# Four edits to a two-layer encoder kernel: a sum order, a prologue order, the diagonal of the row scales, and the value projection of two heads

## The chip, the cores and the metric

One core of a Trainium2 chip runs the whole program in one launch. Its engines are PE (TensorE, the matrix engine), DVE (VectorE), ACT (ScalarE), POOL (GpSimd) and SP (SyncE, which here only starts transfers). Each engine works through its own instruction stream in order and waits at semaphores for the others. The metric is device time in microseconds (us) of the one core, the median of several executions.

## What is computed

The reference takes a sequence of 512 tokens of 1024 features and applies two layers. In the first the mixer is multi-head latent attention (MLA, 16 heads in 8 pairs, chunk-causal), in the second an mLSTM matrix memory (4 heads of 128 query and key features and 256 value features). Behind each mixer stands a feed-forward network (FFN).

```python
for i in range(DEPTH):                       # DEPTH = 2
    hn = rms_norm(x, norm_mix[i])
    y = mla_mixer(hn, ...) if i == 0 else mlstm_mixer(hn, ...)
    x = x + y
    x = x + sqrelu_mlp(rms_norm(x, norm_ffn[i]), ffn_w1[i], ffn_w2[i])

def mlstm_mixer(h, w_in, w_if, b_if, head_norm, w_o):
    q, k, v, o_pre = jnp.split(h @ w_in, [hq, 2 * hq, 2 * hq + hv], axis=-1)
    gates = (h @ w_if + b_if).astype(jnp.float32)
    ...
def sqrelu_mlp(h, w1, w2):
    return jnp.square(jax.nn.relu(h @ w1)) @ w2
```

## The kernel before

**Splits.** Every large product runs in fp32r. Each factor is split into a high part (a cast, usually on ACT) and a low part (a subtraction, on DVE or POOL), and one product becomes three matmuls on PE (`mm3`): high by high, high by low, low by high. A weight is loaded by a transfer into `wr` or `tw`, cast into `wh` and subtracted into `wl`. So each weight passes a transfer, ACT, and DVE or POOL before PE uses it.

**Stages.** The program runs MLA from 0 to about 245 us, the first FFN to about 578, the mLSTM to about 790, and the second FFN to the end. Tokens lie in four blocks of 128, features in eight blocks of 128. In the FFNs and in the MLA the engines keep the order in which the code was written; in most of the mLSTM a scheduler orders the instructions of each engine.

**The MLA prologue.** The string `START` names the work on the first pairs of heads one unit at a time, and each engine takes its share in that order. A unit is a letter, a pair and a token block. W splits a pair's weights (cast on ACT, low part on DVE for the queries and on POOL for the keys and values). P projects (15 matmuls of 256 columns; a small p is the same into another bank). A squares, B makes the statistics (on POOL the small operations `sm` and `scr`), C scales into the tile `f` (two heads on DVE, the rotary half of the keys on POOL). X turns `f` (four transposes on PE, tile `tp`), x splits the result. S, s, M, E and N are scores and softmax of the first head. e, R, r, g and h make and turn the low-rank inputs of a token block. Behind the string comes a loop with its own fixed order, which begins with T0, the turn of the first head's probabilities.

**The FFN.** The second matrix of the FFN is multiplied in chunks by a scheme of seven products on quarter blocks (a Strassen scheme). Its right factors are sums of quarters of the weight; the kernel forms them in transfers that add to what lies in memory (`s_sum`, `l_sum`, all issued from POOL). For the last chunk the factors t1 to t4 lie in two tiles named `z`, which are first filled with the quarter b12 and then take one or more added quarters. t4 takes three, b11, b22 and b21, one behind the other. The left factors are four subtractions on POOL (`z<-z`, x4). The products of a chunk are added to the residual rows `x` by DVE (`y_add`). The last two products of the last chunk, numbers 5 and 6, use t3 and t4, split into the tiles `zw`. Between their halves PE turns the finished rows `x` for the next stage (`mm<-cst,x`), which DVE and ACT scale into `xg`.

**The mLSTM.** The values of a head are projected with 256 columns (264 for head 0, whose weight `w_v0` holds the gates as well), from two weight tiles per head. `rows_sb` spreads the norms of the tokens over all partitions: it makes a diagonal from them and multiplies it by ones.

Of the kernel before, what the change touches and what calls it, by code (L numbers as in the profile page):

```python
# [61 lines left out]
def trunk(ctx: ExitStack, tc, a, yT, dbg=None):  # L62
# [33 lines left out]
    def tmp(dt=F32):  # L96
        return ph[0].tile([P, 512], dt, tag="t", bufs=tb[0], name=nm("t"))
# [87 lines left out]
            c = slice(off + k * stride, off + k * stride + m)  # L185
            mm3(out, hi[:, c], lo[:, c], rhs[k][0], rhs[k][1], k == 0, k == n - 1)

    def rows(r):

        dg = tmp()  # L190
        for t in range(NB):
            nc.vector.tensor_scalar_mul(dg[:, t * P:(t + 1) * P], ident, r[:, t:t + 1])
        ps = ps_tp()
        pe.matmul(ps, lhsT=ones, rhs=dg, start=True, stop=True)
        return ps

# [59 lines left out]
    def mla(mp):  # L256
# [340 lines left out]
                 "T": p_bank, "t": p_split, "V": pv, "o": o_split}  # L597
        ORDER = ("S0 s0 P0 S1 S2 T0 X0 s1 T1 s2 D1 A0 T2 P1 M0 E0 t0 B0 t1 t2 E2 E3 A1 E1 V0 x0 X1 V1 V2 W0 V3 N0 C0 B1 x1 o0")

        START = ("W00 Z00 Z01 g00 e00 g01 Z02 R00 h00 r00 e01 Z04 g02 P00 R01 h01 A00 Z03 e02 r01 B00 W10 R02 g03 h02 C00 r02 P01 X00 A01 e03 R03 P02 B01 h03 r03 A02 C01 B02 P03 P10 x00 X01 C02 x01 A03 B03 X02 p11 x02 S01 C03 A10 P12 S00 X03 B10 W20 s01 A11 C10 X10 x03 s00 S02 A12 B11 s02 p13 M00 B12 C11 X11 x10 E00 E02 A13 B13 E01 E03 C12 N00 C13 x11")  # L600
        PRO = {"Z": lambda t: z_mm((((0, 0), (0, 1)), ((1, 0), (1, 1)), ((2, 1), (3, 1)), ((3, 0),), ((2, 0),))[t], range(KD - ZL, KD)), "e": z_out, "R": z_turn, "Q": lambda t: z_turn(t, True), "r": z_split,
               "h": z_rope, "g": z_stat}

# [119 lines left out]
    def ffn(fp, layer, last):  # L723
# [181 lines left out]
        for s_ in range(2, len(units) - 2):  # L905
            u = units[s_]
            if u[0] == "F":
                ps = ps_mm()
                f_mm(ps, u[1])
                ws.pop(u)  # L910
            else:
                post = s_mm(u[1], u[2])
            ahead(s_)
            s_now[0] = s_
            while later and later[0][0] <= s_:
                later.pop(0)[1]()
            if u[0] == "F":
                f_post(ps, u[1])
                if u[1] == 4 * NC - 2:
                    l_load()  # L920
                if s_ < 5:
                    norm.square(s_ - 1, 0)
                    norm.square(s_ - 1, 1)
                    if s_ == 4:
                        idve.reciprocal(r2[:, 0], norm.stat())
                        idve.tensor_scalar_mul(r2[:, 1], r2[:, 0], -1.0)
            else:
                post()
                c, k = u[1], u[2]
                if c == NC - 1:  # L930
                    pass
                elif c == NC - 2:
                    if k == 2:
                        s_load(c + 1, ("b11",))
                    elif k == 3:
                        l_sum(("t1", "b11"), ("t2", "b11"), ("t3", "b22"), ("t4", "b11"))
                    elif k == 5:
                        s_load(c + 1, ("b21", "b22"))
                        l_sum(("t2", "b22"), ("t4", "b22"))
                    elif k == 6:  # L940
# [45 lines left out]
    def mlstm(lp):  # L986
# [16 lines left out]
        def gates(gps):  # L1003
# [45 lines left out]
            nc.vector.tensor_scalar_mul(cs, r, DK ** -0.5)  # L1049
            G["cs"] = cs  # L1050

        for h in range(MH):
            nv = DV + (2 * MH if h == 0 else 0)
            src = a["w_v0"] if h == 0 else a["w_v"][h - 1]
            ws = [load_w(src[c], 4 * nv, nc.gpsimd if h == 0 else nc.vector) for c in range(2)]
            vh, vl = vt[2 * (h % 2)], vt[2 * (h % 2) + 1]
            nc.gpsimd.memset(vh.bitcast(F32)[:, :, DV:], 1.0)
            nc.gpsimd.memset(vl.bitcast(F32)[:, :, DV:], 0.0)
            gps = []
            for t in range(NB):  # L1060
                tk = slice(t * P, (t + 1) * P)
                ps = ps_mm()
                for k in range(KD):
                    hi, lo = ws[k // 4]
                    c = slice((k % 4) * nv, (k % 4 + 1) * nv)
                    mm3(ps[:, :nv], xg[k][0][:, tk], xg[k][1][:, tk], hi[:, c], lo[:, c], k == 0, k == KD - 1,
                        ipe if h == 0 else pe)
                if h == 0 and t == 0:
                    iact.on = True
                    for do in norm.tail:  # L1070
                        do()
                    for i in range(2):
                        norm.square(2 + i, 0)
                    iact.on = False
                    roots(1)
                nc.scalar.activation(vh[:, t, 0:DV], ps[:, 0:DV], AF.Copy, scale=r[:, t:t + 1])
                nc.vector.scalar_tensor_tensor(vl[:, t, 0:DV], ps[:, 0:DV], r[:, t:t + 1],
                                               vh.bitcast(F32)[:, t, 0:DV], op0=mult, op1=sub)
                if h == 0:
                    gs = small(2 * MH)  # L1080
                    nc.vector.tensor_copy(gs, ps[:, DV:nv])
                    gps.append(gs)
            if h == 0:
                gates(gps)
                R = rows_sb(r)
# [122 lines left out]
def _layout(i):  # L1208
    def f(n):
        return np.asarray(i[n], dtype=np.float32)  # L1210

    def tiles(w):

        k, m = w.shape
        return w.reshape(k // P, P, m // P, P).transpose(2, 1, 0, 3).reshape(m // P, P, k)

    def cols(w):

        k, m = w.shape
# [60 lines left out]
```

## Time and profile before

| | |
|---|---|
| Median of 3 runs | 1130.61 us (1129.76 to 1131.3) |
| The profiled execution, its own time | 1130.33 us |
| Its span, first to last instruction | 1128.6 us |
| PE busy | 1107.3 us, 98% |
| DVE, ACT, POOL busy | 68%, 50%, 32% |
| Mean granted TensorE clock | 0.995 of full speed |

The span leaves 1.7 us around it. A row of a timeline gives the start, the length, the engine, the line, the operation, the tile written and the tiles read, their size, and how many like instructions stand together; in square brackets is the idle time of the engine ahead of it and what ended that. Line 80 is a helper that records instructions in order, so most rows carry it and the tiles tell the place. Matmuls overlap, so the spacing of their starts says more than their length.

### The profile page before, as it was taken

To read this page: it belongs to the slowest core of one execution; us is meant where nothing else is said; L and a number is where in the kernel's file an instruction comes from. 1 tells how busy PE (TensorE), PEld (TensorE's weight loads), DVE (VectorE), ACT (ScalarE), POOL (GpSimd) and SP (SyncE) were. 2 spreads that over 40 slices of the span, in tenths; PEclk is the share of its full clock that TensorE was granted. 3 is DMA by queue.
4 is the path that set the end of the run, shared out by engine and by line. 5 is a ranking of instruction groups with operands and counts; after the bars stand their busy time and mean duration, and the time that the engine had idled before them with its cause. 6 is when DMAs were issued, how large, how long until landed. Compare 5 with 4: busy or idle time off the path is not lost.

```text
span 1128.6 us, 15807 instructions
## 1 busy us (share of the span) xinstructions
PE 1107.3 (98%) x5790; PEld 949.1 (84%) x5790; DVE 763.3 (68%) x1308; ACT 568.0 (50%) x1004; POOL 363.4 (32%) x481
## 2 busy tenths in 40 slices
PE   9899999999999999999999999999999999999998
PEld 8889988888888888888798898888888888888876
DVE  5689997455676776776776465554476776767567
ACT  4478876437444544444465344332654545444442
POOL 3567785203332323324330011000323224224250
PEclk9899999999999999999999999999999999999999
DMA  9201021455666676575923223222675575666575
GB/s 323 72 25 48 20 76 38 131 170 127 170 151 149 165 154 146 151 174 149 203 71 102 86 58 92 81 90 81 197 170 130 159 180 131 164 168 139 160 153 127
DMA packets 44669, 146.23 MB, mean 130 GB/s; under 512 B 4912, under 2 KB 8368, under 8 KB 44592
## 3 DMA queue, kind: packets, MB, share of 16 engines
q1 hardware_dynamic: 34512, 108.52, 30.6%
q0 software_dynamic: 10080, 36.70, 19.2%
q8 instruction: 46, 0.75, 0.3%
q14 instruction: 31, 0.25, 0.1%
HBM read 143.11 MB, written 2.10 MB: 129 GB/s over the span
## 4 chain that ended last, share of the span: by engine, by line
PE 90%; DMA 3%; DVE 3%; POOL 2%; ACT 1%; issue 1%; SPq 0%; ACTq 0%; DVEq 0%; POOLq 0%
PE mm L80 40%; PE tp L80 34%; PE mm L178 4%; PE mm L177 4%; PE mm L176 4%; PE po L80 3%; DMA z<-in_w 1%; DMA wr<-in_w_z 1%; DVE x L80 1%; PE tp L178 1%; PE tp L177 1%; PE tp L176 1%; DMA t<-in_x 1%; POOL z L80 0%; POOL x L80 0%
## 5 line engine op out<-in xcount | busy, mean ns | idle before, releaser
L80 PE MATMUL mm<-xg,wh 128*128 128x512 f32 (+1 forms) x1088 | 318.9, 377 | 0.0
L80 POOL TENSOR_TENSOR z<-z 128x256 f32<-128x256 f32 x128 | 145.1, 1153 | 348.3 <-ACT z L80 345.8
L80 PEld LDWEIGHTS mm<-xg,wh 128*128 128x128 f32 x1088 | 200.1, 188 | 37.5
L80 PE MATMUL mm<-xg,wl 128*128 128x512 f32 (+1 forms) x544 | 204.9, 377 | 0.0
L80 DVE TENSOR_TENSOR wl<-tw,wh 128x1024 fp32r<-128x1024 f32 x104 | 134.5, 1293 | 87.9 <-ACT wh L80 87.9
L80 PE MATMUL tp<-wh,hh 128*128 128x512 f32 x424 | 165.3, 390 | 4.7 <-DVE x L80 4.7
L80 PE MATMUL tp<-wh,hl 128*128 128x512 f32 x424 | 165.0, 389 | 0.0
L80 PE MATMUL tp<-wl,hh 128*128 128x512 f32 x424 | 165.0, 389 | 0.0
L80 DVE TENSOR_TENSOR wl<-wr,wh 128x1024 fp32r<-128x1024 f32 (+1 forms) x72 | 94.0, 1306 | 102.1 <-ACT wh L80 102.1
L80 DVE SCALAR_TENSOR_TENSOR x<-tp,r,x 128x512 f32<-128x512 f32 (+1 forms) x223 | 155.2, 735 | 2.6 <-PE tp L80 2.5
L80 ACT ACTIVATE t<-mm 128x512 f32<-128x512 f32 (+3 forms) x97 | 54.3, 559 | 185.5 <-PE mm L80 179.5
L80 ACT CAST wh<-tw 128x1024 fp32r<-128x1024 f32 x104 | 108.9, 1047 | 40.5 <-DMA tw<-in_w 23.7
L80 PEld LDWEIGHTS mm<-xg,wl 128*128 128x128 f32 x544 | 102.4, 188 | 18.9 <-DVE wl L80 0.4
L80 PEld LDWEIGHTS tp<-wh,hh 128*128 128x128 f32 x424 | 79.6, 188 | 22.6 <-issue 3.5
L80 ACT CAST wh<-wr 128x1024 fp32r<-128x1024 f32 (+1 forms) x74 | 79.0, 1067 | 29.9 <-PE tp L80 25.5
L80 PEld LDWEIGHTS tp<-wh,hl 128*128 128x128 f32 x424 | 79.6, 188 | 16.6
L80 PEld LDWEIGHTS tp<-wl,hh 128*128 128x128 f32 x424 | 79.6, 188 | 16.5
L80 POOL DMA_DIRECT2D tw<-in_w x56 | 49.1, 876 | 124.4 <-DVE wl L80 112.4
L166 DVE TENSOR_TENSOR wl<-wr,wh 128x1024 fp32r<-128x1024 f32 (+1 forms) x39 | 45.7, 1173 | 56.3 <-ACT wh L162 55.5
L162 ACT CAST wh<-wr 128x1024 fp32r<-128x1024 f32 (+2 forms) x42 | 41.9, 1001 | 63.1 <-PE mm L177 31.6
L80 ACT ACTIVATE hh<-z 128x1024 fp32r<-128x1024 f32 x32 | 34.0, 1064 | 71.5 <-POOL z L80 71.5
L80 PE MATMUL mm<-wh,big 128*128 128x256 f32 (+1 forms) x256 | 58.2, 306 | 0.0
(286 smaller groups left out, 2096.5 us busy)
## 6 DMA issues: line engine op xcount, KB each, us to landing
wr<-in_w SPq DMA_DIRECT2D x64, 512.0 KB, 3.7
tw<-in_w SPq DMA_DIRECT2D x62, 512.0 KB, 4.2
tw<-in_w POOLq DMA_DIRECT2D x56, 512.0 KB, 5.7
z<-in_w POOLq DMA_DIRECT2D x14, 512.0 KB, 7.7
wr<-in_w_qkv SPq DMA_DIRECT2D x8, 640.0 KB, 3.9
wr<-in_w_oa SPq DMA_DIRECT2D x8, 512.0 KB, 3.6
z<-in_w SPq DMA_DIRECT2D x8, 512.0 KB, 7.3
wr<-in_w_mo SPq DMA_DIRECT2D x8, 512.0 KB, 3.6
```

The lines of the kernel that those rows point to most:

```text
L80: return lambda *args, **kw: tc.keep_in_program_order(f(*args, **kw)) if self.on else f(*args, **kw)
L162: act.copy(hi[:, :n], raw[:, :n])
L166: dve.tensor_sub(lo[:, :n], raw[:, :n], hi[:, :n].bitcast(F32))
L176: pe.matmul(out, lhsT=lh, rhs=rh, start=start, stop=False)
L177: pe.matmul(out, lhsT=lh, rhs=rl, start=False, stop=False)
L178: pe.matmul(out, lhsT=ll, rhs=rh, start=False, stop=stop)
```

## The change

It has four parts. In `START` the weight split W10 moves from ahead of R02 to behind e03; P02 and R03 now stand ahead of X00; p13 moves from behind s02 to between X03 and X10; W20 moves from behind B10 to behind S02. In both FFNs t4's first added quarter, b11, is issued behind t2's b22 instead of two units earlier, and its second quarter, b22, one unit later (in the chunk ahead of the last the products come in the order 0, 1, 2, 3, 5, 4, 6, so what stands at k == 4 is issued behind what stands at k == 5). `rows_sb` splits the norms and makes two diagonals and two fp32r products where there was one fp32 product. In the mLSTM the values of heads 2 and 3 are projected together with 512 columns from four weight tiles, and the low part of `w_v0` is formed on DVE where it was formed on POOL.

```diff
-    def rows(r):
-        dg = tmp()
         for t in range(NB):
-            nc.vector.tensor_scalar_mul(dg[:, t * P:(t + 1) * P], ident, r[:, t:t + 1])
+            c = slice(t * P, (t + 1) * P)
+            nc.vector.tensor_scalar_mul(dh[:, c], ident, rh[:, t:t + 1])
+            nc.scalar.activation(dl[:, c], ident, AF.Copy, scale=rl[:, t:t + 1])
         ps = ps_tp()
-        pe.matmul(ps, lhsT=ones, rhs=dg, start=True, stop=True)
+        pe.matmul(ps, lhsT=ones_r, rhs=dh, start=True, stop=False)
+        pe.matmul(ps, lhsT=ones_r, rhs=dl, start=False, stop=True)
...
-                        l_sum(("t1", "b11"), ("t2", "b11"), ("t3", "b22"), ("t4", "b11"))
+                        l_sum(("t1", "b11"), ("t2", "b11"), ("t3", "b22"))
                     elif k == 5:
                         s_load(c + 1, ("b21", "b22"))
-                        l_sum(("t2", "b22"), ("t4", "b22"))
+                        l_sum(("t2", "b22"), ("t4", "b11"))
+                    elif k == 4:
+                        l_sum(("t4", "b22"))
...
         for h in range(MH):
-            nv = DV + (2 * MH if h == 0 else 0)
-            src = a["w_v0"] if h == 0 else a["w_v"][h - 1]
-            ws = [load_w(src[c], 4 * nv, nc.gpsimd if h == 0 else nc.vector) for c in range(2)]
             vh, vl = vt[2 * (h % 2)], vt[2 * (h % 2) + 1]
+            if h < 2:
+                nv = DV + (2 * MH if h == 0 else 0)
+                src = a["w_v0"] if h == 0 else a["w_v1"]
+                ws = [load_w(src[c], 4 * nv) for c in range(2)]
...
+            if h == 2:
+                z = [ps_mm() for _ in range(3)] + [pp.tile([P, 512], F32, tag="po", bufs=1, name=nm("po"))]
+                for j in range(4):
+                    w = load_w(a["w_v23"][j], D)
+                    for t in range(NB):
+                        for k in (2 * j, 2 * j + 1):
+                            o_mm(z[t], w, k, t, xg)
+                for t in range(NB):
+                    for n in range(2):
+                        v_out(2 + n, t, z[t][:, n * DV:(n + 1) * DV])
```

The order of the instructions changes at three places that matter below. The first is POOL in the MLA prologue, where pair 1 and pair 2 meet. `f_831` is the rotary half of C10, `wl_836` (`wl_879` in the changed kernel) is the low part of W20, `wl_1221` that of the next pair, and `f_873` (`f_889`) is C11's. Before:

```order
L80 TENSOR_TENSOR scr_371<-sm_828,nhalf 128x4
L80 TENSOR_TENSOR wl_836<-wr_372,wh_835 128x512
L80 TENSOR_TENSOR f_831<-kk,scr_371 128x2x64
L80 TENSOR_TENSOR wl_1221<-wr_947,wh_1220 128x512
L80 TENSOR_TENSOR sm_870<-sm_870,off 128x4
L80 TENSOR_TENSOR scr_371<-sm_870,nhalf 128x4
L80 TENSOR_TENSOR sm_898<-sm_898,off 128x4
L80 TENSOR_TENSOR scr_371<-sm_898,nhalf 128x4
L80 TENSOR_TENSOR f_873<-kk,scr_371 128x2x64
```

and now:

```order
L80 TENSOR_TENSOR scr_371<-sm_828,nhalf 128x4
L80 TENSOR_TENSOR f_831<-kk,scr_371 128x2x64
L80 TENSOR_TENSOR wl_879<-wr_372,wh_878 128x512
L80 TENSOR_TENSOR wl_1221<-wr_947,wh_1220 128x512
L80 TENSOR_TENSOR sm_886<-sm_886,off 128x4
L80 TENSOR_TENSOR scr_371<-sm_886,nhalf 128x4
L80 TENSOR_TENSOR sm_898<-sm_898,off 128x4
L80 TENSOR_TENSOR scr_371<-sm_898,nhalf 128x4
L80 TENSOR_TENSOR f_889<-kk,scr_371 128x2x64
```

The low part of W20 stands behind `f_831`, which X10 turns. Both weight splits still stand ahead of the statistics of B11 and B12 and of C11's `f`.

The second is POOL at the end of the first FFN; the second FFN has the same. `z_5646` holds t1 and t2, `z_5649` t3 and t4, `z_5642` is the left factor, and the `wl` rows are splits of the mLSTM's first weights. Before:

```order
L80 DMA z_5646<-in_w 128x1024 x2
L80 DMA z_5649<-in_w 128x1024 x2
L80 TENSOR_TENSOR z_5642<-z_5642 128x256 x4
L80 DMA z_5646<-in_w 128x1024
L80 DMA z_5649<-in_w 128x1024 x2
L166 TENSOR_TENSOR wl_6024<-wr_6021,wh_6023 128x1056
L166 TENSOR_TENSOR wl_6030<-wr_6027,wh_6029 128x1056
L166 TENSOR_TENSOR wl_6237<-wr_6234,wh_6236 128x1024
```

and now:

```order
L80 DMA z_5646<-in_w 128x1024 x2
L80 DMA z_5649<-in_w 128x1024
L80 TENSOR_TENSOR z_5642<-z_5642 128x256 x4
L80 DMA z_5646<-in_w 128x1024
L80 DMA z_5649<-in_w 128x1024 x3
L166 TENSOR_TENSOR wl_6247<-wr_6244,wh_6246 128x1024
```

One of the two transfers ahead of the subtractions, t4's first, now stands with t4's other two behind them and behind t2's; the two splits of `w_v0` are gone from POOL.

The third is DVE at the same place. `zw_5869` and `zw_5886` are the low parts of t3 and t4, `x` rows are `y_add`s, and `tp_5797` and `tp_5798` are PE's banks for the two halves of products 3, 5 and 6 of the chunk. Before:

```order
L80 TENSOR_TENSOR zw_5869<-z_5649,zw_5869 128x1024
L80 SCALAR_TENSOR_TENSOR x_3191<-tp_5797,r_737_3422,x_3191 128x512
L80 SCALAR_TENSOR_TENSOR x_3195<-tp_5798,r_737_3422,x_3195 128x512
L80 TENSOR_TENSOR zw_5886<-z_5649,zw_5886 128x1024
L80 SCALAR_TENSOR_TENSOR x_3191<-tp_5817,r_737_3422,x_3191 128x512
L80 SCALAR_TENSOR_TENSOR x_3195<-tp_5818,r_737_3422,x_3195 128x512
L80 SCALAR_TENSOR_TENSOR x_3199<-tp_5797,r_737_3422,x_3199 128x512
L80 SCALAR_TENSOR_TENSOR xg_5899<-mm_5919,cst,xg_5891 128x256
```

and now:

```order
L80 TENSOR_TENSOR zw_5869<-z_5649,zw_5869 128x1024
L80 SCALAR_TENSOR_TENSOR x_3191<-tp_5797,r_737_3422,x_3191 128x512
L166 TENSOR_TENSOR wl_6024<-wr_6021,wh_6023 128x1056
L80 SCALAR_TENSOR_TENSOR x_3195<-tp_5798,r_737_3422,x_3195 128x512
L80 TENSOR_TENSOR zw_5886<-z_5649,zw_5886 128x1024
L166 TENSOR_TENSOR wl_6030<-wr_6027,wh_6029 128x1056
L80 SCALAR_TENSOR_TENSOR x_3191<-tp_5817,r_737_3422,x_3191 128x512
L80 SCALAR_TENSOR_TENSOR x_3195<-tp_5818,r_737_3422,x_3195 128x512
L80 SCALAR_TENSOR_TENSOR x_3199<-tp_5797,r_737_3422,x_3199 128x512
L80 SCALAR_TENSOR_TENSOR xg_5899<-mm_5919,cst,xg_5891 128x256
```

The two splits of `w_v0` (`wl_6024`, `wl_6030`) now stand between the `y_add`s. Each reads a `wh` that ACT casts; on ACT, whose order is unchanged there, the cast of `wh_6023` stands right behind the cast of t4's `zw_5886`.

## Rows read from the trace of the kernel before

**Rows 1.** Page, part 1: busy time, share of the span, instructions.

```profile
PE 1107.3 (98%) x5790; PEld 949.1 (84%) x5790; DVE 763.3 (68%) x1308; ACT 568.0 (50%) x1004; POOL 363.4 (32%) x481
```

**Rows 2.** Timeline of PE, 42 to 75 us: start, length, instruction, idle before.

```profile
44.75 0.73 PE L80 MATMUL tp<-cst,f 128*128 128x128 f32 x2 [1.94 <-DVE f L80]
47.42 0.69 PE L80 MATMUL tp<-cst,f 128*128 128x128 f32 x2 [1.93 <-POOL f L80]
...
48.82 2.91 PE L80 MATMUL mm<-big,big 128*128 128x256 f32 x12
...
52.03 1.60 PE L80 MATMUL mm<-big,big 128*128 128x256 f32 x12
...
68.64 0.73 PE L80 MATMUL tp<-cst,f 128*128 128x128 f32 x4
...
73.71 0.63 PE L80 MATMUL tp<-cst,x 128*128 128x128 f32 x4 [0.41 <-DVE big L80]
```

**Rows 3.** Windows: us, busy PE, PEld, DVE, ACT, POOL, clock, DMA, GB/s.

```profile
45.00:52.00 7.00, 5.07 (x24) 4.77 (x24) 4.59 (x16) 1.78 (x6) 4.87 (x19) 0.51 0.29 94
```

**Rows 4.** Timeline of ACT and POOL, 59 to 67 us.

```profile
59.93 1.35 ACT L80 CAST wh<-wr 128x1280 fp32r<-128x1280 f32 x1
...
64.41 1.29 POOL L80 TENSOR_TENSOR wl<-wr,wh 128x512 fp32r<-128x512 f32 x1
...
65.93 1.01 POOL L80 TENSOR_TENSOR scr<-sm,nhalf 128x4 f32<-128x4 f32 x1
```

**Rows 5.** Timeline of PE in the mLSTM stage, 600 to 617 us.

```profile
600.31 1.10 PE L194 MATMUL tp<-t,ones 128*128 128x512 f32 x2
...
601.48 0.39 PE L176 MATMUL mm<-xg,wh 128*128 128x512 f32 x1
...
602.17 0.39 PE L176 MATMUL mm<-xg,wh 128*128 128x512 f32 x1
...
616.22 0.28 PE L176 MATMUL mm<-wh,xg 128*128 128x256 f32 x1
...
616.69 0.28 PE L177 MATMUL mm<-wl,xg 128*128 128x256 f32 x1
```

**Rows 6.** Timeline of ACT and POOL at the end of the first FFN.

```profile
546.53 0.63 ACT L80 ACTIVATE z<-t 128x512 f32<-128x512 f32 x1
...
547.48 0.86 POOL L80 DMA_DIRECT2D z<-in_w  x1 [2.89 <-DMA z<-in_w]
...
548.05 4.85 POOL L80 TENSOR_TENSOR z<-z 128x256 f32<-128x256 f32 x4
...
555.74 0.86 POOL L80 DMA_DIRECT2D z<-in_w  x1 [2.03 <-DMA z<-in_w]
...
561.41 0.86 POOL L80 DMA_DIRECT2D z<-in_w  x1 [4.81 <-DMA z<-in_w]
```

**Rows 7.** Timeline of ACT, DVE and PE, 566 to 579 us.

```profile
566.80 1.05 ACT L80 CAST zw<-z 128x1024 fp32r<-128x1024 f32 x1 [2.99 <-DMA z<-in_w]
...
568.75 1.21 DVE L80 TENSOR_TENSOR zw<-z,zw 128x1024 fp32r<-128x1024 f32 x1
...
569.88 2.20 DVE L80 SCALAR_TENSOR_TENSOR x<-tp,r,x 128x512 f32<-128x512 f32 x3
...
571.49 0.71 PE L80 MATMUL tp<-zw,hh 128*128 128x512 f32 x2
...
578.13 0.28 PE L80 MATMUL mm<-wh,xg 128*128 128x264 f32 x1
```

**Rows 8.** Timeline of POOL, ACT and PE, end of the second FFN.

```profile
1097.69 1.77 POOL L80 DMA_DIRECT2D z<-in_w  x2
...
1106.13 0.86 POOL L80 DMA_DIRECT2D z<-in_w  x1 [6.66 <-DMA z<-in_w]
...
1111.73 1.06 ACT L80 CAST zw<-z 128x1024 fp32r<-128x1024 f32 x1 [3.06 <-DMA z<-in_w]
...
1117.83 1.47 PE L80 MATMUL mm<-cst,x 128*128 128x128 f32 x12
```

More of the change, by code (lines that the diff above doesn't have):

```diff
@@ L186, in proj, with rows_sb @@
             mm3(out, hi[:, c], lo[:, c], rhs[k][0], rhs[k][1], k == 0, k == n - 1)
-    def rows(r):
-        dg = tmp()
+    def rows_sb(r):
+        rh, rl = small(NB), small(NB)
+        nc.vector.tensor_copy(rh.bitcast(F32R), r)
+        nc.vector.tensor_sub(rl, r, rh)
+        dh, dl = tmp(F32R), tmp(F32R)
         for t in range(NB):
-            nc.vector.tensor_scalar_mul(dg[:, t * P:(t + 1) * P], ident, r[:, t:t + 1])
+            c = slice(t * P, (t + 1) * P)
+            nc.vector.tensor_scalar_mul(dh[:, c], ident, rh[:, t:t + 1])
+            nc.scalar.activation(dl[:, c], ident, AF.Copy, scale=rl[:, t:t + 1])
         ps = ps_tp()
-        pe.matmul(ps, lhsT=ones, rhs=dg, start=True, stop=True)
-        return ps
-    def rows_sb(r):
-        ps = rows(r)
+        pe.matmul(ps, lhsT=ones_r, rhs=dh, start=True, stop=False)
+        pe.matmul(ps, lhsT=ones_r, rhs=dl, start=False, stop=True)
         R = ph[0].tile([P, T], F32, name=nm("R"))
@@ L598, in mla @@
         ORDER = ("S0 s0 P0 S1 S2 T0 X0 s1 T1 s2 D1 A0 T2 P1 M0 E0 t0 B0 t1 t2 E2 E3 A1 E1 V0 x0 X1 V1 V2 W0 V3 N0 C0 B1 x1 o0")
-        START = ("W00 Z00 Z01 g00 e00 g01 Z02 R00 h00 r00 e01 Z04 g02 P00 R01 h01 A00 Z03 e02 r01 B00 W10 R02 g03 h02 C00 r02 P01 X00 A01 e03 R03 P02 B01 h03 r03 A02 C01 B02 P03 P10 x00 X01 C02 x01 A03 B03 X02 p11 x02 S01 C03 A10 P12 S00 X03 B10 W20 s01 A11 C10 X10 x03 s00 S02 A12 B11 s02 p13 M00 B12 C11 X11 x10 E00 E02 A13 B13 E01 E03 C12 N00 C13 x11")
+        START = ("W00 Z00 Z01 g00 e00 g01 Z02 R00 h00 r00 e01 Z04 g02 P00 R01 h01 A00 Z03 e02 r01 B00 R02 g03 r02 C00 P01 h02 e03 W10 A01 P02 R03 X00 B01 h03 r03 A02 C01 B02 P03 P10 x00 X01 C02 x01 A03 B03 X02 p11 x02 S01 C03 A10 P12 S00 X03 B10 s01 A11 s00 p13 C10 X10 x03 S02 W20 A12 B11 s02 M00 B12 C11 X11 x10 E00 E02 A13 B13 E01 E03 C12 N00 C13 x11")
         PRO = {"Z": lambda t: z_mm((((0, 0), (0, 1)), ((1, 0), (1, 1)), ((2, 1), (3, 1)), ((3, 0),), ((2, 0),))[t], range(KD - ZL, KD)), "e": z_out, "R": z_turn, "Q": lambda t: z_turn(t, True), "r": z_split,
@@ L1050, in gates, with v_out @@
             G["cs"] = cs
+        def v_out(h, t, ps):
+            vh, vl = vt[2 * (h % 2)], vt[2 * (h % 2) + 1]
+            nc.scalar.activation(vh[:, t, 0:DV], ps, AF.Copy, scale=r[:, t:t + 1])
+            nc.vector.scalar_tensor_tensor(vl[:, t, 0:DV], ps, r[:, t:t + 1], vh.bitcast(F32)[:, t, 0:DV],
+                                           op0=mult, op1=sub)
         for h in range(MH):
-            nv = DV + (2 * MH if h == 0 else 0)
-            src = a["w_v0"] if h == 0 else a["w_v"][h - 1]
-            ws = [load_w(src[c], 4 * nv, nc.gpsimd if h == 0 else nc.vector) for c in range(2)]
             vh, vl = vt[2 * (h % 2)], vt[2 * (h % 2) + 1]
-            nc.gpsimd.memset(vh.bitcast(F32)[:, :, DV:], 1.0)
-            nc.gpsimd.memset(vl.bitcast(F32)[:, :, DV:], 0.0)
+            if h < 2:
+                nv = DV + (2 * MH if h == 0 else 0)
+                src = a["w_v0"] if h == 0 else a["w_v1"]
+                ws = [load_w(src[c], 4 * nv) for c in range(2)]
+                nc.gpsimd.memset(vh.bitcast(F32)[:, :, DV:], 1.0)
+                nc.gpsimd.memset(vl.bitcast(F32)[:, :, DV:], 0.0)
             gps = []
-            for t in range(NB):
+            for t in range(NB) if h < 2 else ():
                 tk = slice(t * P, (t + 1) * P)
@@ L1075, in mlstm @@
                     roots(1)
-                nc.scalar.activation(vh[:, t, 0:DV], ps[:, 0:DV], AF.Copy, scale=r[:, t:t + 1])
-                nc.vector.scalar_tensor_tensor(vl[:, t, 0:DV], ps[:, 0:DV], r[:, t:t + 1],
-                                               vh.bitcast(F32)[:, t, 0:DV], op0=mult, op1=sub)
+                v_out(h, t, ps[:, 0:DV])
                 if h == 0:
@@ L1253, in _layout @@
     o["w_v0"] = np.stack([cols(v0[:D // 2]), cols(v0[D // 2:])])
-    o["w_v"] = np.stack([np.stack([cols(wv[:D // 2, h * DV:(h + 1) * DV]), cols(wv[D // 2:, h * DV:(h + 1) * DV])])
-                         for h in range(1, MH)])
+    o["w_v1"] = np.stack([cols(wv[:D // 2, DV:2 * DV]), cols(wv[D // 2:, DV:2 * DV])])
+    o["w_v23"] = wv[:, 2 * DV:].reshape(4, 2, P, 512).transpose(0, 2, 1, 3).reshape(4, P, D)
     o["w_mo"] = tiles(w_in[:, 2 * hq + hv:])
```

## The prediction

> **What bounds the kernel now.** I read the page first: PE is busy for 1107.3 of 1128.6 us [rows 1]. So only two things can move the time: the length of PE's own work, and the 21 us in which PE stands still. Then I read the timeline of PE at the four places that the change touches, and behind each gap the timelines of the engines that ended it.
>
> In the MLA prologue PE waits 1.94 us for DVE's and 1.93 us for POOL's part of the first `f`; the projection behind them, 15 matmuls from 48.82 to 52.03, takes 3.2 us [rows 2], because the granted clock is 0.51 there, the lower of its two levels, 1.2 GHz [rows 3]. In the mLSTM the matmuls follow each other without a gap [rows 5]. At the end of the first FFN PE does not wait, but ACT does: the cast of t4 stood 2.99 us for the last added quarter and ran at 566.80 [rows 7]. There the chain of three added quarters on POOL is the latest thing, with little slack behind it. So my estimate depends more on when t4 lands than on any matmul.
>
> **Merged value projection.** 192 matmuls of 256 columns become 96 of 512. From 616.22 to 616.69 four of the small ones start, 0.1175 us apart; from 601.48 to 602.17 three of the large ones, 0.23 us apart [rows 5]. Over longer runs I read 0.227. 192 x 0.1175 - 96 x 0.227 = 22.6 - 21.8 = **-0.8 us**. The bounds are -0.9 and, if PE waits once for the fourth bank, 0. The Trainium skill ("TensorE: Matmul & The Clock Gate", section "Wait — 56ns, not 53.3ns?") gives a warm matmul a fixed cost of about 2.5 ns beyond its columns; by that the 96 matmuls saved would be worth 0.24 us, while the rows show more per matmul, and the sum goes by the rows.
>
> **Row scales.** The fp32 product runs as two passes, and from its start at 600.31 to the next matmul but one at 601.48 lie 1.17 us [rows 5], one other matmul of 0.23 among them: 0.94. Two fp32r products of 512 columns cost 0.45. **-0.5 us**. The ten small operations that it adds on DVE and ACT stand in a stretch where PE has the next projections to do. Without that cover they would cost about 2 us, but PE showed no wait.
>
> **Prologue.** Now P02 (1.8 us at the full clock) and R03 stand ahead of X00 and fill the gaps. P01 ends at 42.8, P02 at 44.6; R03 needs DVE's rows of the last block, about 46.6, and ends at 47.5; X00 ends at 48.2. P03, P10 then follow at the full clock, and X01 starts at about 52.0 where it started at 55.6: 3.6 us earlier. Then the next limit comes. X03 ends near 58.2; ACT splits it (0.6) and casts two pairs' weights of 1.35 each [rows 4], to 61.3; POOL makes the last low part (1.29), then two statistics of about 1.2 (1.01 in the `scr`) and `f`: 65.3. So X11 ends at 65.6, where it ended at 69.1 (it began at 68.64 [rows 2]): still 3.5 earlier. But with p13 moved ahead PE has nothing left from about 61 to 64.6. A smaller pair of gaps, 1.94 and 1.93, was followed by the low clock [rows 2, 3]. The stretch from X11 to T0, 68.64 to 73.71 [rows 2], would then pay about 1.3. I take 3.5 - 1.3 = **-2.2 us**. Bounds: -3.7 without the low clock, -0.5 if the low clock lasts twice as long and DVE and ACT, whose work moves up too, come late once more. Behind T0 the fixed loop keeps PE full, so nothing is returned later.
>
> **t4 and the end of the first FFN.** This is the largest term. Before, the subtractions ran at 548.05 behind the issue of t4's first quarter, which had waited 2.89 us for the tile to land [rows 6]. Now they start when ACT's square ends, 547.2 [rows 6], 0.9 earlier, and take 4.85. Only then t4's first sum is issued, at about 552.7, next to t2's; before it went out at 547.48. The three sums must follow each other. In the second FFN a pair issued together at 1097.69 let the next sum start at 1106.13, some 7.6 us after the second of the pair was issued [rows 8]. Alone a step took 5.67 (555.74 to 561.41) and the last 5.39, to the cast at 566.80 [rows 6, 7]. So t4 lands at 552.7 + 7.5 + 5.7 + 5.4 = 571.3, 4.5 us later than before.
>
> What is queued behind it: on ACT the cast of t4, and right behind it that of `w_v0`, to 573.4 (1.05 each). On DVE the low part of `w_v0` now stands ahead of a `y_add`; it waits for that cast, runs 1.25 (the like operation took 1.21 [rows 7]) and then the `y_add`, 0.7 (three took 2.20 [rows 7]), ends at 575.4. PE needs that bank for the second half of product 5, which started at 571.49 [rows 7]: 3.9 us late. Behind the `y_add` DVE does t4's low part, the second split of `w_v0` and two `y_add`s: 575.4 + 1.2 + 1.25 + 1.4 = 579.1. The turns of those rows on PE wait for them. From 571.49 to the mLSTM's first projection at 578.13 PE had 6.64 us of work [rows 7]; in it 1.8 us before these turns are done by 577.3, and PE waits from 577.3 to 579.1. So the projection starts at 575.4 + 6.64 + 1.8 = 583.9: **+5.8 us**. Bounds: with three steps of 5.4 t4 lands at 568.9 and the cost is +3.4; with the slower start of the pair +6.4. The earlier subtractions shorten two small waits of PE on the way, which gains nothing, as t4 decides.
>
> **The clock behind it.** PE would idle 3.9 and 1.8 us within 8 us, more than in the prologue where the clock fell. The price from rows: 15 matmuls took 3.21 us instead of 1.76 [rows 2], **+1.4 us**. Bounds 0 and +2.2 (the whole of 47.4 to 51.8 at half speed).
>
> **The second FFN.** By the same steps the subtractions start at 1090.9, t4's sums at 1096.4, and t4 lands at 1096.4 + 7.5 + 5.7 + 5.6 = 1115.2, where its cast ran at 1111.73 [rows 8]. No weight split stands on DVE here. Cast to 1116.3, low part to 1117.5, two `y_add`s to 1118.9; the turns that wait for them stood at 1118.2, the third part of the group at 1117.83 [rows 8]: **+0.9 us**. Bounds: -0.5, if the shorter wait for the earlier subtractions counts (PE stood 2.4 us for them), and +1.2.
>
> **Sum.** -0.8 - 0.5 - 2.2 + 5.8 + 1.4 + 0.9 = +4.6 on the profiled execution's own time, 1130.33 (1.7 above its span, and 0.3 below the median): 1134.9 us. About 0.2%, 2.3 us, can be told from no change.
>
> **Rivals.**
> *t4 lands in time, and the kernel is faster.* Without a wait for the quarter between the sums, or with steps of 4.8 us, t4 lands by 567. Then the new splits on DVE delay only the later `y_add`s, by two splits less the slack, +1.0 at the first FFN, and the second FFN gains what its subtractions gain, 1.3: 1130.3 - 0.8 - 0.5 - 2.2 + 1.0 - 1.3 = 1126.5. For it: much of the other traffic on the queues is done by then. Against: no step in these rows was under 5.3, three in a row need 16. It decides at a landing of 567. Chance 0.15.
> *The two ends cancel.* The prologue keeps its 3.5 without a low clock, the steps are short (+4.0) and the clock holds: -1.3 - 3.6 + 4.0 + 0.5 = -0.4, 1129.9; half of it gives 1132. Chance 0.25.
> *The prologue gives nothing either.* Its gain is eaten by POOL, on which two splits still stand ahead of B11; all else as summed: 1130.3 + 4.6 + 1.7 = 1136.6, with the longer low clock 1138. Chance 0.15.
> *My sum*, 1133 to 1136: 0.45.
>
> **How the numbers follow.** The range leaves out the last part of each side case: 1127.5 to 1137.5. The first rival is faster (0.15) with a little of the second (0.03); the rest of the second is the same, or just above; the others are slower: 0.18, 0.22, 0.60.
>
> **What would show it.** In the profile after: POOL's subtractions near 547 and t4's last landing near 571; on ACT a wait of some 7 us ahead of t4's cast; on DVE waits ahead of the `w_v0` split; two waits of PE before 580 and a low clock behind them; in the prologue no wait of 1.9 us near 45 but one of 3 to 4 ahead of X11. I am wrong if t4's cast runs before 568, or if DVE's order lets the `y_add` pass.

## The result, and the profile after

The changed kernel takes 1138.74 us (median of 4 runs, 1137.36 to 1139.94), the kernel before 1130.95 beside it (1129.76 to 1132.84): a ratio of 1.0065, 95% interval 1.005 to 1.0079, so 5.7 to 8.9 us slower. The forecast was +4.6 with a range up to 1137.5; the direction is right, and the time lies 1.2 us above the range. The profiled execution of the changed kernel took 1139.94, the slowest of the four, with a span of 1138.1 against 1128.6. So the two profiled executions lie 9.5 us apart, and the medians 7.8.

The busy times on the page of the kernel after, for [rows 1]:

```profile
PE 1109.0 (97%) x5694; PEld 945.4 (83%) x5694; DVE 765.7 (67%) x1312; ACT 568.2 (50%) x1008; POOL 358.5 (32%) x475
```

and the head of its list of PE's waits (what waited for whom, total, times, longest):

```profile
PE tp L80 <- DVE x L80: 8.8, 6, 5.7
PE tp L80 <- DVE f L80: 4.2, 2, 3.9
PE mm L80 <- DVE x L80: 3.3, 3, 2.5
```

PE has about the same work as before and waits more; the longest wait is 5.7 us. I place that by cutting both timelines at five events of PE, which can be found in every kernel here: the second projection of the prologue (P01), the turn T0, the first half of the last chunk's product 5 in the first FFN, the mLSTM's first projection, and the 16 turns at the start of the second FFN. The table gives the us between them, from the starts of those rows:

| | before | after | difference |
|---|---|---|---|
| P01 to T0 (prologue) | 32.94 | 31.88 | -1.1 |
| T0 to product 5 (MLA, first FFN) | 496.05 | 495.97 | -0.1 |
| product 5 to mLSTM (first boundary) | 8.37 | 16.95 | +8.6 |
| mLSTM | 212.48 | 210.91 | -1.6 |
| second FFN to the end | 337.99 | 341.00 | +3.0 |

Their sum is +8.9; the other 0.6 lies ahead of P01, whose start lies between 40.8 and 44.2 us in the traces of this document, with either `START`. One pair of executions does not price every row. Over all these traces the prologue takes 32.4 to 32.9 us with the old `START` and 31.9 to 33.2 with the whole new one, and the second FFN 337.1 to 339.3 with the old sums and 338.6 to 341.6 with the late ones. The first boundary is steady: 8.4 to 8.5 in every kernel with the sums and the split as before.

**Prologue.** PE of the kernel after, to be held against [rows 2]:

```profile
43.37 2.05 PE L80 MATMUL mm<-big,big 128*128 128x256 f32 x12
...
46.91 0.60 PE L80 MATMUL tp<-cst,f 128*128 128x128 f32 x4
...
66.50 0.59 PE L80 MATMUL tp<-cst,f 128*128 128x128 f32 x2 [3.90 <-DVE f L80]
...
73.27 0.60 PE L80 MATMUL tp<-cst,x 128*128 128x128 f32 x4
```
and a row of its table of windows (us, busy of PE, PEld, DVE, ACT and POOL, granted clock, share of DMA, GB/s):

```profile
69.00:74.00 5.00, 5.00 (x31) 4.82 (x31) 3.04 (x11) 1.50 (x6) 3.10 (x7) 0.77 0.00 0
```

The waits of 1.94 and 1.93 us are gone: P02 starts at 43.37 behind P01, X00's four turns stand together at 46.91. X11 waits 3.90 us instead, and behind that the granted clock is 0.77 where it was 1.00 from 69 to 74. Two more waits of the kernel before are gone, ahead of X10, and with them a second stretch of low clock, in which p13 ran and which [rows 2, 3] do not show:

```profile
63.30 0.59 PE L80 MATMUL tp<-cst,f 128*128 128x128 f32 x2 [1.48 <-DVE f L80]
64.50 0.44 PE L80 MATMUL tp<-cst,f 128*128 128x128 f32 x2 [0.62 <-POOL f L80]
```
```profile
65.40:69.00 3.60, 3.60 (x20) 3.56 (x19) 3.06 (x12) 1.32 (x6) 3.04 (x6) 0.53 0.41 159
```

So the edit leaves one stretch of low clock where there were two. X11 waits for DVE's `f` (66.10), which waits for the statistics on POOL (the `scr` of 65.06), and until 64.8 POOL is busy with two weight splits:

```profile
61.54 3.28 POOL L80 TENSOR_TENSOR wl<-wr,wh 128x512 fp32r<-128x512 f32 x2 [1.27 <-ACT wh L80]
```

**First boundary.** POOL, for [rows 6]:

```profile
547.07 4.63 POOL L80 TENSOR_TENSOR z<-z 128x256 f32<-128x256 f32 x4 [2.70 <-ACT z L80]
551.65 1.77 POOL L80 DMA_DIRECT2D z<-in_w  x2
560.24 0.86 POOL L80 DMA_DIRECT2D z<-in_w  x1 [6.82 <-DMA z<-in_w]
566.56 0.86 POOL L80 DMA_DIRECT2D z<-in_w  x1 [5.46 <-DMA z<-in_w]
```

The subtractions start at 547.07, 1.0 earlier, and t4's first sum stands behind them, as the second of the pair at 551.65. The steps of the chain end at 560.24 and 566.56 and with the cast on ACT at 572.92. ACT, DVE and PE, for [rows 7]:

```profile
572.92 1.04 ACT L80 CAST zw<-z 128x1024 fp32r<-128x1024 f32 x1 [9.64 <-DMA z<-in_w]
573.88 1.07 ACT L162 CAST wh<-wr 128x1056 fp32r<-128x1056 f32 x1
...
574.97 1.26 DVE L166 TENSOR_TENSOR wl<-wr,wh 128x1056 fp32r<-128x1056 f32 x1 [7.35 <-ACT wh L162]
...
576.95 1.22 PE L80 MATMUL tp<-zw,hh 128*128 128x512 f32 x2 [5.75 <-DVE x L80]
...
577.99 0.82 ACT L80 ACTIVATE xg<-mm,cst 128x256 fp32r<-128x256 f32 x2
...
579.11 2.06 DVE L80 SCALAR_TENSOR_TENSOR x<-tp,r,x 128x512 f32<-128x512 f32 x3
...
581.09 0.87 DVE L80 SCALAR_TENSOR_TENSOR xg<-mm,cst,xg 128x256 fp32r<-128x256 f32 x2
...
582.10 0.63 PE L80 MATMUL mm<-cst,x 128*128 128x128 f32 x4 [0.99 <-DVE xg L80]
...
586.19 0.28 PE L80 MATMUL mm<-wh,xg 128*128 128x264 f32 x1
```
and a window, columns as above:

```profile
576.00:580.00 4.00, 3.05 (x8) 2.37 (x9) 4.00 (x6) 2.82 (x6) 1.83 (x1) 0.57 0.41 131
```

The reader can follow the queue down the rows. ACT waits 9.64 us for t4; the cast of `w_v0` comes behind it at 573.88; DVE has waited 7.35 us for that cast with the split of `w_v0` at the head of its queue; the `y_add` behind it lets PE go on at 576.95, after 5.75 us, at a granted clock of 0.57. One more wait follows, 0.99 us at 582.10: PE's next turn needs a bank that DVE's `xg` must have read. That `xg` starts at 581.09 without idle time, as soon as DVE is through with the second split of `w_v0` and three `y_add`s; ACT's `xg`, at 577.99, was done long before.

**Second FFN.** For [rows 8], POOL, ACT and PE:

```profile
1102.05 1.78 POOL L80 DMA_DIRECT2D z<-in_w  x2
...
1111.53 0.86 POOL L80 DMA_DIRECT2D z<-in_w  x1 [7.70 <-DMA z<-in_w]
...
1117.17 0.86 POOL L80 DMA_DIRECT2D z<-in_w  x1 [4.78 <-DMA z<-in_w]
...
1122.87 1.04 ACT L80 CAST zw<-z 128x1024 fp32r<-128x1024 f32 x1 [9.20 <-DMA z<-in_w]
...
1125.89 0.38 PE L80 MATMUL mm<-cst,x 128*128 128x128 f32 x1 [2.47 <-DVE x L80]
```
and the window of its end, columns as above:

```profile
1122.00:1130.00 8.00, 5.24 (x23) 4.17 (x22) 5.09 (x7) 2.12 (x3) 0.00 (x0) 0.79 0.21 66
```

t4 is cast at 1122.87. PE has reached the turns that need it and stands 2.47 us, and the clock behind it is 0.79.

**mLSTM.** The two products of the row scales are 0.31 us apart, and the next matmul follows 0.23 behind:

```profile
609.52 0.47 PE L199 MATMUL tp<-t,ones_r 128*128 128x512 f32 x1
609.83 0.39 PE L200 MATMUL tp<-t,ones_r 128*128 128x512 f32 x1
610.06 0.39 PE L177 MATMUL mm<-xg,wh 128*128 128x512 f32 x1
```

### The profile page after: what moved, and what is told of

Read it like the earlier page. It is cut to its first block, busy times and chain, and to the rows that moved or that the text cites. A ratio compares the mean times of both kernels' runs of the same rounds, so it can differ in the third digit from the quotient of the medians.

```text
span 1138.1 us, 15615 instructions
## 1 busy us (share of the span) xinstructions
PE 1109.0 (97%) x5694; PEld 945.4 (83%) x5694; DVE 765.7 (67%) x1312; ACT 568.2 (50%) x1008; POOL 358.5 (32%) x475
## 4 chain that ended last, share of the span: by engine, by line
PE 85%; POOL 4%; issue 3%; DMA 3%; DVE 3%; ACT 1%; SPq 0%; POOLq 0%; ACTq 0%; DVEq 0%
PE mm L80 38%; PE tp L80 31%; PE mm L178 3%; PE mm L176 3%; PE mm L177 3%; PE po L80 3%; DMA z<-in_w 1%; POOL z L80 1%; DMA wr<-in_w_z 1%; POOL scr L80 1%; DVE x L80 1%; PE tp L178 1%; PE tp L177 1%; PE tp L176 1%; POOL wl L80 1%
## 5 line engine op out<-in xcount | busy, mean ns | idle before, releaser
L80 DVE TENSOR_TENSOR wl<-wr,wh 128x1024 fp32r<-128x1024 f32 (+1 forms) x72 | 94.0, 1305 | 101.6 <-ACT wh L80 101.5
L166 DVE TENSOR_TENSOR wl<-wr,wh 128x1024 fp32r<-128x1024 f32 (+2 forms) x41 | 48.3, 1177 | 58.0 <-ACT wh L162 57.5
```

Of the source, the lines that this page charges most:

```text
L80: return lambda *args, **kw: tc.keep_in_program_order(f(*args, **kw)) if self.on else f(*args, **kw)
L166: dve.tensor_sub(lo[:, :n], raw[:, :n], hi[:, :n].bitcast(F32))
```

## The experiments

Each kernel was timed in five rounds beside the kernel before; the median of that stands next to each, and the 95% interval of the ratio in brackets. A difference in us is worked out from the ratio where "by the ratio" is said, else from the medians.

**The sums of t4 alone, in both FFNs.**

```diff
# the kernel before, with:
-l_sum(("t1", "b11"), ("t2", "b11"), ("t3", "b22"), ("t4", "b11"))
+l_sum(("t1", "b11"), ("t2", "b11"), ("t3", "b22"))
...
-l_sum(("t2", "b22"), ("t4", "b22"))
+l_sum(("t2", "b22"), ("t4", "b11"))
+elif k == 4:
+    l_sum(("t4", "b22"))
```

> The kernel before with one edit, the later sums of t4 in both FFNs. Theory (t4's landing carries the loss): t4's last sum lands about 6 us later at both FFN ends. At the first, the split of w_v0 stays on POOL and no y_add queues behind it, so the turns wait only for t4's cast and low part: +3 to +4.5 there, and about +3 at the end of the second FFN: 1131 + 6.5 = 1137 to 1138.5. Rival (the split of w_v0 on DVE carries it, t4's lateness is mostly covered): no more than +3 in all, 1131 to 1134.

1140.08 us against 1131.53, ratio 1.0078 (1.0065 to 1.009), so 8.8 us by the ratio. The first theory holds in kind, and its 1137 to 1138.5 is still too small: the sums by themselves cost no less than the whole change.

**The changed kernel with the old sums.**

```diff
# the kernel after, with:
-l_sum(("t1", "b11"), ("t2", "b11"), ("t3", "b22"))
+l_sum(("t1", "b11"), ("t2", "b11"), ("t3", "b22"), ("t4", "b11"))
...
-l_sum(("t2", "b22"), ("t4", "b11"))
-elif k == 4:
-    l_sum(("t4", "b22"))
+l_sum(("t2", "b22"), ("t4", "b22"))
```

> The changed kernel with the sums of t4 issued as before; the other three edits stay. Theory: t4 lands near 566.7 again, the split of w_v0 on DVE then delays the y_adds by about 1, the mLSTM keeps its 1.4, the prologue next to nothing: 1129.5 to 1131. Rival (the split on DVE costs by itself, whatever t4 does): 1133 or more. Rival (the prologue or the merged projection lose): 1136 or more.

1131.71 against 1131.53, ratio 1.0002 (0.9993 to 1.0011). Without the late sums the other edits come out at nothing, 0.7 above the upper end of the theory and below both rivals. In the profile the mLSTM keeps its 1.6, and the first boundary takes 12.76 us where it took 8.37: PE waits there 0.87, 0.33 and 0.99 us for DVE, on which the split of `w_v0` stands, and the clock behind is 0.73 from 580 to 584.

**The changed kernel with the split of `w_v0` on POOL.**

```diff
# the kernel after, with:
-ws = [load_w(src[c], 4 * nv) for c in range(2)]
+ws = [load_w(src[c], 4 * nv, nc.gpsimd if h == 0 else nc.vector) for c in range(2)]
```

> The changed kernel with the low part of w_v0 formed on POOL as before; t4's sums stay late. Theory: the y_adds pass, product 5's second half starts at 571.5 again and the first boundary costs 3 to 4.5 instead of 8.2: 1134 to 1135.5. Rival (t4 alone sets the boundary, the split on DVE is hidden in its wait): unchanged, 1138 to 1139.

1137.09 against 1131.53, ratio 1.0049 (1.0037 to 1.0062). Product 5's second half starts on time, at 571.09, but the boundary still takes 15.65 us, 1.3 less than the changed kernel's, in an execution in which t4 also came 1.7 earlier beside PE's work. So with t4 late the split on DVE adds little: 1.8 by the ratios, which is not clear of noise, as the two intervals overlap. The time lies between the theory and the rival: the theory named the wrong queue for most of the cost.

**The new `START` alone, and each of its halves.**

```diff
# alone: both pieces of the string. First half alone:
-B00 W10 R02 g03 h02 C00 r02 P01 X00 A01 e03 R03 P02 B01
+B00 R02 g03 r02 C00 P01 h02 e03 W10 A01 P02 R03 X00 B01
# second half alone:
-X03 B10 W20 s01 A11 C10 X10 x03 s00 S02 A12 B11 s02 p13 M00
+X03 B10 s01 A11 s00 p13 C10 X10 x03 S02 W20 A12 B11 s02 M00
```

> The kernel before with the new START string alone. Theory after the result: the prologue's earlier part gains, the wait ahead of X11 gives it back: 1130.0 to 1131. The prediction's term: -2.2, 1128.8.

> The kernel before with the new START up to X00 alone (W10 behind e03, P02 and R03 ahead of X00); p13 and W20 stay where they were. Theory (the earlier part gains, the later part gives it back): X01 starts 2.5 to 3.5 earlier, p13 still fills the time ahead of X11: 1128.5 to 1129.5. Rival (whatever comes earlier on PE waits for POOL's chain to X11 anyway): 1131 to 1132.

> The kernel before with the new START behind X00 alone (p13 ahead of X10, W20 behind S02). Theory: p13 no longer fills the wait ahead of X11, which becomes 3 us or more, with the low clock behind it: +1 to +2, 1132.5 to 1133.5. Rival (X10's early turn pays for it): no change, 1131 to 1132.

Alone: 1131.57 against 1131.53, ratio 1.0001 (0.9992 to 1.001). First half: 1127.89 against 1131.82, 0.9968 (0.9956 to 0.9981). Second half: 1133.65, 1.0024 (1.0012 to 1.0037). So by the ratio the edit holds a gain of 3.6 (2.2 to 5.0) and a loss of 2.7 (1.4 to 4.2). Each goes the way its theory said, and a little beyond its range. PE of the kernel with the first half alone:

```profile
61.29 0.59 PE L80 MATMUL tp<-cst,f 128*128 128x128 f32 x2 [1.42 <-DVE f L80]
62.50 0.44 PE L80 MATMUL tp<-cst,f 128*128 128x128 f32 x2 [0.62 <-POOL f L80]
...
65.54 0.59 PE L80 MATMUL tp<-cst,f 128*128 128x128 f32 x2
...
70.80 0.60 PE L80 MATMUL tp<-cst,x 128*128 128x128 f32 x4
```
and a window of the same kernel:

```profile
65.00:69.00 4.00, 3.19 (x23) 2.67 (x22) 3.40 (x15) 4.00 (x14) 3.44 (x7) 1.00 0.03 12
```

p13's 15 matmuls stand between 63.4 and 65.5, X11 begins at 65.54 without a wait of its own, the clock stays at 1.00 where it was 0.53 before, and T0 starts 29.20 us behind P01, 3.7 sooner than before. In the profile of the second half alone X11 waits 3.90 us again, and T0 starts 36.20 us behind P01, 3.3 later than before. Moved ahead of X10, p13 no longer fills that time, and the two weight splits on POOL still stand ahead of B11.

**The sums in one FFN.**

```diff
# the kernel before; second FFN alone (for the first, `not last` and the names turned round):
-l_sum(("t1", "b11"), ("t2", "b11"), ("t3", "b22"), ("t4", "b11"))
+l_sum(("t1", "b11"), ("t2", "b11"), ("t3", "b22"), *(() if last else (("t4", "b11"),)))
...
-l_sum(("t2", "b22"), ("t4", "b22"))
+l_sum(("t2", "b22"), ("t4", "b11" if last else "b22"))
+elif k == 4 and last:
+    l_sum(("t4", "b22"))
```

> The kernel before with t4's later sums in the second FFN alone. Theory: its end pays 2.5 to 3, with the low clock in it, so 1134 to 1134.5, and the first boundary pays the other 5.5 to 6 of the two together. The prediction's term: +0.9, 1132.4.

> The kernel before with t4's later sums in the first FFN alone. Theory: what the both-FFNs run cost less what the second alone cost, 8.6 - 1.4 = 7, to 1138 to 1139, though nothing of the split stands on DVE: behind t4's cast stand the casts of w_v0 and w_mq and the scaling of the turned rows on ACT. Rival (without the split on DVE the first boundary costs 3 to 4.5): 1134.5 to 1136.

The second FFN alone: 1132.68 against 1131.82, 1.0012 (1.0003 to 1.0021), +1.4 by the ratio. The first alone: 1138.18 against 1130.63, 1.0062 (1.0049 to 1.0076), +7.0 by the ratio. The second is nearer to the prediction's +0.9 than to the +3.0 that the profile after had suggested; in its own profile t4 is cast at 1115.33, where the forecast had it land at 1115.2. The first falls to the theory. There nothing of the split stands on DVE, and still PE waits. ACT, DVE and PE of the kernel with the first FFN's sums late:

```profile
572.03 1.05 ACT L80 CAST zw<-z 128x1024 fp32r<-128x1024 f32 x1 [8.25 <-DMA z<-in_w]
...
575.05 0.33 PE L80 MATMUL mm<-cst,x 128*128 128x128 f32 x1 [1.52 <-DVE x L80]
...
575.20 2.00 ACT L162 CAST wh<-wr 128x1056 fp32r<-128x1056 f32 x2
...
577.11 2.28 ACT L80 ACTIVATE xg<-mm,cst 128x256 fp32r<-128x256 f32 x6
577.96 0.88 DVE L80 SCALAR_TENSOR_TENSOR xg<-mm,cst,xg 128x256 fp32r<-128x256 f32 x2 [1.64 <-ACT xg L80]
...
578.98 1.08 PE L80 MATMUL mm<-cst,x 128*128 128x128 f32 x4 [2.72 <-DVE xg L80]
...
585.87 0.28 PE L80 MATMUL mm<-wh,xg 128*128 128x264 f32 x1
```

The turns go on at 575.05, 3 us behind t4's cast. Then PE stands 2.72 us more for a bank that DVE's `xg` must empty (577.96); DVE waits for ACT's `xg` (577.11); and ACT has the casts of two further weights at 575.20 ahead of it, because everything in its queue was held by t4's cast. Of this queue on ACT the prediction had only the first cast of `w_v0`.

**The split of `w_v0` on DVE alone.**

```diff
# the kernel before, with:
-ws = [load_w(src[c], 4 * nv, nc.gpsimd if h == 0 else nc.vector) for c in range(2)]
+ws = [load_w(src[c], 4 * nv) for c in range(2)]
```

> The kernel before with w_v0's low part on DVE alone. Theory (the split stands in DVE's order ahead of a y_add and waits for the cast behind t4's, also when t4 lands on time): +1 to +3, 1132.5 to 1134.5. Rival (with t4 on time it is hidden): 1131 to 1132.

1134.38 against 1130.63, ratio 1.0034 (1.0022 to 1.0047). The theory holds, at or above its upper end. In its profile t4 is cast on time (570.05, 3.1 us ahead of product 5, as before), and the boundary takes 10.21 us instead of 8.37; that explains 1.8 of the 3.8 by the ratio. Where the rest falls this profile doesn't show. In the profile of the changed kernel with the old sums, which has the same split, t4 is cast 2.2 us ahead of product 5, PE waits longer, the low clock follows, and the boundary costs 4.4: so the price differs from execution to execution.

**The mLSTM's two edits alone.**

```diff
# the kernel after, with the START string and the sums of before, and:
-ws = [load_w(src[c], 4 * nv) for c in range(2)]
+ws = [load_w(src[c], 4 * nv, nc.gpsimd if h == 0 else nc.vector) for c in range(2)]
```

> The kernel before with the joined value projection of heads 2 and 3 and the two fp32r products for the row scales alone; w_v0 is split on POOL as before. Theory (the prediction's two terms, -0.8 and -0.5): 1130 to 1130.6. Rival (the mLSTM stage waits elsewhere and gives it back): 1131.5.

1128.47 against 1130.63, ratio 0.9979 (0.997 to 0.9988): 2.4 us less by the ratio (1.4 to 3.4), more than the theory had. The stage itself takes 210.92 us instead of 212.48, 1.56 less; the two terms were 1.3. The row scales have 0.4 of it (0.54 from the first product to the next matmul in the profile after, 0.94 before), which leaves 1.16 for the joined projection, above the 0.8 worked out. The estimate of 0.24 that follows from the fixed cost per matmul in the Trainium skill ("TensorE: Matmul & The Clock Gate", section "Wait — 56ns, not 53.3ns?") does not agree; the measurement decides.

**Matmuls in PE's wait.** The product is read by nothing and changes no output.

```diff
# the kernel after, between the turns and the second half of product 5:
+if not last:
+    warm = pp.tile([P, 512], F32, tag="po", bufs=1, name=nm("warm"))
+    for _ in range(22):
+        ipe.matmul(warm, lhsT=hs[C, 0][0][:, 0, :P], rhs=ws["P", C, 5][0][:, :512], start=True, stop=True)
```

> The changed kernel with 22 matmuls of 512 columns, whose product nothing reads, in PE's 5.7 us wait at the end of the first FFN. They take 5.0 us at the full clock, so they fit in the wait. Theory (the low clock behind the wait costs 1.4 by the prediction's term, part of it hidden by DVE): the clock stays up and the time falls by 0.7 to 1.5, to 1137 to 1138. Rival (DVE and ACT set the pace behind the wait, whatever PE's clock): unchanged, 1138.5 to 1139.

1140.71 against 1131.82, ratio 1.0081 (1.0068 to 1.0095), where the changed kernel has 1.0065: no gain. PE of the kernel with the filler:

```profile
572.24 5.27 PE L80 MATMUL warm<-zw,hh 128*128 128x512 f32 x22
577.34 0.61 PE L80 MATMUL tp<-zw,hh 128*128 128x512 f32 x2
...
582.00 0.63 PE L80 MATMUL mm<-cst,x 128*128 128x128 f32 x4 [0.99 <-DVE xg L80]
```
and its windows:

```profile
576.00:580.00 4.00, 3.50 (x18) 2.69 (x16) 4.00 (x6) 3.38 (x7) 1.93 (x1) 1.00 0.42 131
...
584.00:588.00 4.00, 4.00 (x19) 3.45 (x19) 3.01 (x8) 2.27 (x7) 0.00 (x0) 0.71 0.08 31
```

The filler keeps the clock at 1.00 through 576 to 580, where it was 0.57 in the changed kernel, but PE then waits again for DVE (0.99 us at 582.00), and the clock falls later, to 0.71 from 584 to 588. The boundary takes 17.20 us, not less than 16.95. From t4's cast to the turn behind this wait lie 9.2 us in both kernels (572.92 to 582.10, and 572.81 to 582.00), so up to there DVE's queue behind the cast sets the pace, and the low clock of the changed kernel costs nothing. From that turn to the mLSTM's first projection lie 4.1 us in the changed kernel and 5.7 with the filler, without a further wait: the low clock that comes later costs 1.6.

**The parts that gain, together.** The first half of `START`, the joined projection and the row scales, and all else as before.

```diff
# the kernel of the mLSTM's two edits, with:
-B00 W10 R02 g03 h02 C00 r02 P01 X00 A01 e03 R03 P02 B01
+B00 R02 g03 r02 C00 P01 h02 e03 W10 A01 P02 R03 X00 B01
```

> The kernel before with the new START up to X00, the joined value projection and the row scales in fp32r; t4's sums, p13, W20 and the split of w_v0 as before. Theory (the parts add): 1131.5 - 3.6 - 1.3 = 1126 to 1127.2. Rival (they share a wait): 1127.5 to 1128.5.

1125.35 against 1130.63, ratio 0.9948 (0.9936 to 0.9961): 5.3 us faster than the kernel before, or 5.9 by the ratio, where the parts alone give 3.6 and 2.4. The parts add. In the profile the clock is 0.50 from 63.2 to 66.6, behind waits of 1.41 and 0.62 us ahead of X10, and T0 starts 29.94 us behind P01, for 29.20 in the kernel with the first half of `START` alone.

## Why the prediction was wrong in size

The sum gave 1134.9 and the time was 1138.74. Of these 3.8 us 0.6 is the base: the sum stands on a profiled execution of 1130.33, and the kernel before has a median of 1130.95 beside the changed one. The rest lies in the terms (us; measured by the ratio, each part alone):

| | forecast | measured |
|---|---|---|
| mLSTM | -1.3 | -2.4 |
| prologue | -2.2 | +0.1 |
| first boundary, with the clock | +7.2 | +7.0 for the sums, about 1.8 more with the split |
| second FFN | +0.9 | +1.4 |

**What held.** The sign, and the step that carries it: t4's three sums behind the subtractions make its landing late, ACT and DVE queue behind it, PE waits at the first boundary. The second half of product 5 waits on exactly the `y_add` that was named. The second FFN's +0.9 measured +1.4 alone (0.3 to 2.4). In the mLSTM the way was right and the size too small: the spacing of the small matmuls was read from four starts, 0.1175 us, and over all 288 of the stage it is 0.1214.

**The step that failed most: the prologue, "-2.2".** Alone it measured +0.1 (-0.9 to +1.1). The mechanism was right in both halves: the waits near 45 go, and a wait with the low clock behind it comes ahead of X11. What failed is the time at which X11 can end, which the sum put 24.8 us behind P01 (65.6 and 40.77). Counted from P01, X01 came as forecast, but X03 ended 0.6 later, ACT's two casts 0.7 and POOL's low parts 1.6. The prediction reckoned one low part of 1.29 behind the last cast; when that cast ended, POOL was still in the first of two, and the two took 3.28 together. So X11 ended 26.6 behind P01, where it had ended 28.4 behind it: a gain of 1.8 and not 3.5. From there to T0 it took 5.3 us in the changed kernel and 6.5 in the kernel with the new `START` alone, for 4.6 before: a loss of 0.7 and 1.9, where the sum had 1.3. The prologue gained 1.1 us in the one profile and lost 0.2 in the other.

**The first boundary, "+5.8" and "+1.4".** The profile after has +8.6 for 7.2, and the 1.4 between them lies ahead of t4's cast. It ran at 572.92 for 571.3: the steps on POOL took 6.3 and 6.4 for 5.7 and 5.4 ([rows 6, 7]). That is 3.7 us behind the start of product 5, where the forecast has 1.5; in the other four kernels with the late sums it is 2.0 to 2.3. From the cast to the mLSTM's first projection the profile has 13.3 us, and the forecast 14.0 with its 1.4 for the clock; the low clock filled none of it up to the turn at 582.10, as the run with the filler shows. The second wait of 1.8 ahead of the turns did not come; PE, at the low clock, was late by itself. Instead PE waited 0.99 for DVE's `xg`, which the prediction had left out of the queue.

That the number came near is in part luck. The prediction put the price on the split of `w_v0` on DVE, and the runs show that it is not needed: with the first FFN's sums late and the split on POOL, the way from t4's cast to the projection takes 13.8 us. I had expected 3 to 4.5 there, and it costs 7.0, because ACT's queue behind the same cast holds PE as DVE's does. The split adds about 1.8 when t4 is late, not clear of noise, and 3.8 when it is not.

**The rival that came nearest.** "The prologue gives nothing either" had a chance of 0.15, and the upper of its two times is the number of the prediction nearest to the measured one. Its reason, two splits on POOL ahead of B11, is what the row of 61.54 shows. It added 1.7 to the sum, where leaving out the whole term adds 2.2 (1137.1). That upper time, 1138, lay outside the range, which ended at 1137.5. Two smaller sums are off as well: 575.4 + 1.2 + 1.25 + 1.4 is 579.25 and not 579.1, and from 1118.2 to 1118.9 it is 0.7 and not 0.9; neither changes the result.

**The parts overlap.** By the ratio the sums alone cost 8.8 and the split 3.8, the mLSTM's edits give 2.4, `START` nothing: 10.3. Together it is 7.4. The sums and the split wait at the same place for the same cast; the difference is little more than the intervals allow.

**What stays open.** Why t4's later steps take 6.3 us in one execution and 5.8 in another; what the low clock costs in the prologue and the second FFN; and how the split on DVE comes to 3.8 in the timed runs, between the 1.8 and the 4.4 of two profiled boundaries.

## What to carry to other kernels

A transfer that can only follow another is a chain, and moving its first link behind a long operation moves all of them: look at what the last link releases, and at everything queued behind that on each engine, ACT's scaling and casts too, not only at the operation that waits. Where two queues stand behind the same late transfer, taking the work out of one leaves the other. An order string should be split in halves and timed: here one half gains 3.6 us and the other gives 2.7 back, which the sum hides. Work moved ahead to fill one gap should be looked for in the gap it used to fill. And a stage's gain in one pair of profiles should be held against further traces: the prologue gained 1.1 us in one and nothing in the timed runs.

## What the runs showed of the hardware that was not expected

The granted clock fell behind gaps of quite unequal kind, and not always behind the same ones. In the kernel before it was 0.51 behind two gaps of 1.9 us [rows 2, 3], and 0.53 from 65.4 to 69 behind gaps of 1.48 and 0.62. In the kernel with the first half of `START`, behind gaps of 1.42 and 0.62 us, it stayed at 1.00; in the kernel of the parts that gain, which has the same string, it was 0.50 from 63.2 to 66.6 behind gaps of 1.41 and 0.62. So in these traces the length of the gaps alone does not decide it. After the filler it fell behind gaps of 0.50, 0.33 and 0.99 us (0.86 from 580 to 584, 0.71 from 584 to 588), when no wait over 1 us had gone before it.

A low part of 128x512 on POOL took 2.05 us in the changed kernel and in that with the new `START` alone, where DVE forms one of 128x768 at the same time (both begin within 0.1 us of each other), and 1.27 us in the kernel before, where DVE's had ended. That the one slows the other is not shown by a run of its own.
